# Rotating images by 180 degrees: the first group's load as four transfers of every fourth partition

## The chip, the core and the metric

The kernel runs on one core of one Trainium2 chip. The time is that of the device, in microseconds (us), for one execution; the number compared is the median over runs. A core has compute engines (of which this kernel uses DVE, the vector engine) and sixteen DMA engines that move data between the chip's main memory and the on-chip memory of 128 partitions. Transfers are issued by instructions on SP or on ACT, each of which has a DMA queue of its own; in the profile SP's queue is q1 and ACT's is q10.

## What is computed

Each of 32 x 3 images of 256 x 256 float32 values is turned by 180 degrees:

```python
def reference(x):            # x: (32, 3, 256, 256) float32
    return np.rot90(x, k=2, axes=(-2, -1)).astype(np.float32)
```

As an image lies in memory as 65,536 consecutive values, turning it by 180 degrees is reversing the order of these values. Nothing is calculated; 25.17 MB are read and 25.17 MB are written.

## The kernel before

The 96 images form three groups of 32 (G = 32). Each image is cut into four quarters of E = 16,384 values, so that a group is a tile of 128 partitions x 16,384 values: partition 4n + s holds quarter s of image n. The groups have one tile each, A, Bt and Ct, all resident at once, and there is a scratch tile T of 128 x 2,048.

A quarter is reversed inside its partition by DVE. `swap(t, lo, w)` (line 61) exchanges a stretch of w values at the front with the one at the mirrored place, both reversed, by three copies over T (all through line 52). `inside(t)` does a whole tile with four swaps of J = 2,048. The four quarters of an image must also change places; that is done by the store, whose destination has the quarter index reversed (line 58), so a store has the outer dimensions 32 (images) x 4 (quarters, reversed).

The order of the work is that of the program text:

1. Loads (lines 71 to 75): the first 512 values of every partition of A by ACT, the other 15,872 by SP, then all of Bt and all of Ct by SP. `load` (line 54) is one transfer of 128 rows.
2. DVE reverses most of A: three swaps of 2,048 and one of J - LAST = 896 (lines 78 to 80).
3. SP issues a short store of A's first LEAD = 128 columns (line 81), which are then final.
4. DVE reverses Bt (line 82) and then the remaining LAST = 1,152 values of each half of A (line 83).
5. SP issues the stores of the rest of A and of Bt; DVE reverses Ct; SP issues the store of Ct (lines 84 to 87).

Every store waits on SP for the DVE copies before it, and transfers of one queue are served in the order of issue. The lead store stands in SP's queue behind the load of Ct. The copies are kept in program order; the first copy of a swap reads the end of a partition and the second its front.

Of the kernel before, what the change touches and what calls it, by code (L numbers as in the profile page):

```python
# [2 lines left out]

os.environ.setdefault("NEURON_RT_ULTRASERVER_MODE", "4")

# [4 lines left out]


@with_exitstack
def kernel(
    ctx: ExitStack,
    tc: tile.TileContext,
    x: bass.AP,
    out: bass.AP,
):

    nc = tc.nc
    P = 128

    B, C, H, W = x.shape
    L = H * W
    G = 32
    E = L // 4
    J = E // 8

    x4 = x.rearrange("b c h w -> (b c) (h w)").rearrange(
        "(g n) (s e) -> g (n s) e", n=G, s=4)
    o4 = out.rearrange("b c h w -> (b c) (h w)").rearrange(
        "(g n) (s e) -> g n s e", n=G, s=4)  # L40

    pool = ctx.enter_context(tc.tile_pool(name="slots", bufs=1))
    A = pool.tile([P, E], x.dtype, tag="A")
    Bt = pool.tile([P, E], x.dtype, tag="B")
    Ct = pool.tile([P, E], x.dtype, tag="C")
    T = pool.tile([P, J], x.dtype, tag="T")

    def back(t, lo, hi):
        return t[:, hi - 1:(lo - 1 if lo else None):-1]

    def copy(dst, src):
        tc.keep_in_program_order(nc.vector.tensor_copy(out=dst, in_=src))  # L52

    def load(t, g, lo, hi, queue=nc.sync):
        return queue.dma_start(out=t[:, lo:hi], in_=x4[g][:, lo:hi])  # L55

    def store(t, g, lo, hi):
        return nc.sync.dma_start(
            out=o4[g][:, ::-1, lo:hi], in_=t[:, lo:hi])

    def swap(t, lo, w):
        hi = E - lo - w
        copy(T[:, 0:w], back(t, hi, hi + w))
        copy(t[:, hi:hi + w], back(t, lo, lo + w))
        copy(t[:, lo:lo + w], T[:, 0:w])

    def inside(t):
        for lo in range(0, E // 2, J):
            swap(t, lo, J)

    HEAD = 512
    load(A, 0, 0, HEAD, nc.scalar)
    load(A, 0, HEAD, E)
    load(Bt, 1, 0, E)
    load(Ct, 2, 0, E)
    LAST = 1152
    LEAD = 128
    for lo in range(0, E // 2 - J, J):
        swap(A, lo, J)
    swap(A, E // 2 - J, J - LAST)  # L80
    store(A, 0, 0, LEAD)
    inside(Bt)
    swap(A, E // 2 - LAST, LAST)
    store(A, 0, LEAD, E)
    store(Bt, 1, 0, E)
    inside(Ct)
    store(Ct, 2, 0, E)


# [1 line left out]
_INS = ['x']  # L91
_OUTS = [((32, 3, 256, 256), 'float32')]


# [23 lines left out]
```

## Time and profile before

| what | us |
|---|---|
| median of 3 runs (lowest, highest) | 121.94 (121.89, 122.06) |
| the profiled execution, own time | 122.03 |
| its span, from the first to the last instruction | 120.2 |
| DVE busy | 44.6 |
| issue of A's loads on SP and ACT | 0.73 |
| first copy on A | 22.68 |
| first copy on Bt | 42.10 |
| first copy on Ct | 61.50 |

The span is shorter than the execution's time, as the latter holds what comes before the first and after the last instruction. The profile lists for each DMA queue the packets, the bytes and the time that the packets took as a share of sixteen engines' span. Windows are stretches of the span with the busy time of DVE, the granted clock, the DMA share and the GB/s moved; as the bytes of a packet are counted where it ends, a short window can show more than the engines can move. The chain of waits follows the work that ended last back to what released it. The trace also has one record for each DMA packet with its start, duration, size and queue.

### The profile page before, as it was taken

What the parts mean: (1) busy time and instruction counts of PE and PEld (TensorE: products, weight loads), DVE (VectorE), ACT (ScalarE), POOL (GpSimd) and SP (SyncE); (2) the same over time, 40 slices, a digit from 0 to 9 for tenths busy, and PEclk for the clock granted to TensorE, in tenths of its full rate; (3) what the DMA queues carried; (4) which work ended last, traced back from release to release, by engine and by line L of the source; (5) the groups of instructions that cost most, each with busy time, mean ns of one, the idle gap of its engine ahead of it and who ended that gap; (6) DMA issues with size and microseconds to landing.
All of it is one profiled execution on the core that took longest, in us unless ns stands there. A gap on an engine that the chain in (4) does not pass through costs nothing.

```text
span 120.2 us, 98 instructions
## 1 busy us (share of the span) xinstructions
DVE 44.6 (37%) x39; POOL 0.2 (0%) x4
## 2 busy tenths in 40 slices
DVE  0000000499990099999759999400000000000000
POOL 0000000000000000000000000000000000000000
DMA  9888988899889988998889777988898889888980
GB/s 338 349 349 349 698 349 349 360 654 392 349 349 610 436 349 349 589 458 349 349 368 692 346 346 346 692 349 349 349 698 349 349 349 698 349 349 349 676 371 0
DMA packets 1152, 50.33 MB, mean 419 GB/s; under 512 B 128, under 2 KB 256, under 8 KB 384
## 3 DMA queue, kind: packets, MB, share of 16 engines
q1 hardware_dynamic: 1008, 50.07, 96.7%
q10 hardware_dynamic: 144, 0.26, 0.6%
HBM read 25.17 MB, written 25.17 MB: 419 GB/s over the span
## 4 chain that ended last, share of the span: by engine, by line
DMA 34%; DVE 27%; another core or an unknown queue 2%; issue 1%; SPq 0%; DVEq 0%
DMA Bt<-in_x_dram 34%; DVE T L52 9%; DVE Bt L52 8%; DVE Ct L52 8%; DVE A L52 1%; SPq L55 0%; DVEq L52 0%
## 5 line engine op out<-in xcount | busy, mean ns | idle before, releaser
L52 DVE COPY T<-A 128x2048 f32<-128x2048 f32 (+2 forms) x5 | 5.1, 1014 | 22.8 <-DMA A<-in_x_dram 22.7
L52 DVE COPY T<-Bt 128x2048 f32<-128x2048 f32 x4 | 4.9, 1227 | 6.2 <-DMA Bt<-in_x_dram 6.1
L52 DVE COPY T<-Ct 128x2048 f32<-128x2048 f32 x4 | 4.9, 1227 | 2.0 <-DMA Ct<-in_x_dram 1.9
L52 DVE COPY A<-T 128x2048 f32<-128x2048 f32 (+2 forms) x5 | 5.1, 1013 | 0.2
L52 DVE COPY A<-A 128x2048 f32<-128x2048 f32 (+2 forms) x5 | 5.1, 1013 | 0.2
L52 DVE COPY Bt<-T 128x2048 f32<-128x2048 f32 x4 | 4.9, 1227 | 0.1
L52 DVE COPY Ct<-T 128x2048 f32<-128x2048 f32 x4 | 4.9, 1227 | 0.1
L52 DVE COPY Bt<-Bt 128x2048 f32<-128x2048 f32 x4 | 4.9, 1226 | 0.1
L52 DVE COPY Ct<-Ct 128x2048 f32<-128x2048 f32 x4 | 4.9, 1226 | 0.1
L102 POOL MEMSET const-bfloat16-1.0<- 128x1 bf16 x1 | 0.1, 103 | 0.0
L102 POOL MEMSET const-uint8-127<- 128x1 uint8 x1 | 0.1, 103 | 0.0
L102 POOL MEMSET const-float32-1.0<- 128x1 f32 x1 | 0.1, 100 | 0.0
L102 POOL MEMSET const-float32-0.0<- 128x1 f32 x1 | 0.1, 99 | 0.2 <-issue 0.2
## 6 DMA issues: line engine op xcount, KB each, us to landing
out_dram<-A SPq DMA_DIRECT2D x1, 8128.0 KB, 21.2
A<-in_x_dram SPq DMA_DIRECT2D x1, 7936.0 KB, 21.9
A<-in_x_dram ACTq DMA_DIRECT2D x1, 256.0 KB, 22.1
out_dram<-A SPq DMA_DIRECT2D x1, 64.0 KB, 35.2
Bt<-in_x_dram SPq DMA_DIRECT2D x1, 40.8
Ct<-in_x_dram SPq DMA_DIRECT2D x1, 59.8
out_dram<-Bt SPq DMA_DIRECT2D x1, 39.9
out_dram<-Ct SPq DMA_DIRECT2D x1, 42.8
```

The lines of the kernel that those rows point to most:

```text
L52: tc.keep_in_program_order(nc.vector.tensor_copy(out=dst, in_=src))
L102: nc = _bacc.Bacc("TRN2", target_bir_lowering=False, num_devices=1)
```

## The change

The two loads of A by columns are replaced by four transfers by rows. Transfer i (0 to 3) takes the rows i, i + 4, i + 8 and so on, 32 whole rows of 16,384 values, into the partitions of the same numbers; that is quarter i of every image. Transfers 0 and 2 are issued by SP, 1 and 3 by ACT. The loads of Bt and Ct, the copies and the stores stay as they are.

```diff
-    HEAD = 512
-    load(A, 0, 0, HEAD, nc.scalar)
-    load(A, 0, HEAD, E)
+    SPLIT = 4
+    for i in range(SPLIT):
+        (nc.sync, nc.scalar)[i % 2].dma_start(
+            out=A[i::SPLIT, :], in_=x4[0][i::SPLIT, :])
     load(Bt, 1, 0, E)
     load(Ct, 2, 0, E)
```

In the built program SP then has four load issues ahead of its first store instead of three, and ACT two instead of one. The first copy on A waits for all four transfers (before: for the one by SP, and the second copy for the one by ACT), and so does the lead store; the store of the rest of A waits for DVE alone. All other instructions and their order are the same.

## The prediction

> **What bounds the kernel now.** I read the page's slices first, then the DMA queues, then windows cut at the moments where transfers land, and the chain of waits last.
>
> ```profile
> span 120.2 us, 98 instructions
> DVE 44.6 (37%) x39; POOL 0.2 (0%) x4
> DMA  9888988899889988998889777988898889888980
> ...
> q1 hardware_dynamic: 1008, 50.07, 96.7%
> q10 hardware_dynamic: 144, 0.26, 0.6%
> ```
>
> The only engine that computes is busy for 37% of the span, while packets fill 96.7% + 0.6% of the sixteen DMA engines' time, with zero only in the last slice. The windows (length, DVE busy, clock, DMA share, GB/s) show that nothing slackens between stages:
>
> ```profile
> 5.30:22.70 17.40, 0.02 (x1) 0.00 (x0) 1.00 1.00 431
> 22.70:42.00 19.30, 12.90 (x12) 0.00 (x0) 1.00 1.00 435
> 42.00:61.40 19.40, 17.00 (x15) 0.00 (x0) 1.00 1.01 435
> 61.40:80.80 19.40, 14.72 (x12) 0.00 (x0) 1.00 0.99 429
> 80.80:100.10 19.30, 0.00 (x0) 0.00 (x0) 1.00 1.00 435
> ```
>
> One packet is one row. At 435 GB/s an engine gets 27.2 GB/s, so a row of 65,536 bytes takes 2.41 us; the trace's packet records give a median of 2.418 us. They also give 2.342 us for the 63,488-byte rows of A, 0.084 us for the 2,048-byte heads and 2.401 us for the 65,024-byte rows of A's store. An engine carries 8 rows of each group. Its whole load is 8 x (2.342 + 0.084) + 16 x 2.418 + 8 x (0.027 + 2.401) + 16 x 2.418 = 116.2 us. The first packet starts at 1.77 us; the first rows end between 4.78 and 5.27 us (so the slowest engine is 5.27 - 1.77 - 2.34 = 1.16 us behind an ideal start); the last row of all ends at 119.09, its semaphore arrives at 119.44, and the end of the program follows at 120.2. 1.77 + 1.16 + 116.2 = 119.1: the end is the start of the slowest engine's stream plus its bytes.
>
> ```profile
> 1.18 40.84 DMA Bt<-in_x_dram
> ...
> 59.59 1.82 another core or an unknown queue
> ```
>
> In the chain of waits B's transfer ends at 42.02 (1.18 + 40.84). From there to 59.59 DVE reverses B and the rest of A (15 copies). Then SP issues A's store: 0.63 us of issue, with its first packet at 60.82. The engines finish C between 60.46 and 61.06 and then move the short lead store. So this store arrives just in time: the slowest engine is free at 61.26, 0.44 us after the first packet could start. Whatever delays B by more than that without delaying C becomes a gap.
>
> **The change, part by part.** The durations are of the profiled execution: 122.03 us with a span of 120.2, so 1.8 us lie around the span. The median of the runs is 121.94, 0.09 lower.
>
> Issues: on SP one issue (0.39 us) becomes two, so those of B and C move back by one step (1.18 to 1.65, 1.65 to 2.12). B's rows are not reached before about 21.8 us, where its first packet starts now: some 19 us of A's rows hide the 0.47. Without that cover it would cost 0.47. On ACT one issue (0.38) becomes two; ACT has nothing behind them.
>
> ```profile
> 0.73 0.38 ACTq L55 DMA_DIRECT2D A<-in_x_dram  x1
> 0.73 0.39 SPq L55 DMA_DIRECT2D A<-in_x_dram  x1
> 1.18 0.43 SPq L55 DMA_DIRECT2D Bt<-in_x_dram  x1
> ```
>
> Bytes: none added, none removed. If each new transfer gives each DMA engine 32/16 = 2 rows, an engine gets 4 x 2 x 2.418 = 19.34 us of A instead of 8 x 2.426 = 19.41: -0.07. Two more transfers add two semaphore writes per engine of 0.009 us: +0.02. Sum -0.05.
>
> Interleaving: half of A's rows now stand in ACT's queue. The records show what an engine does with two queues: after its first row it takes one head from q10, then one row from q1, in turn, eight times, at a period of 2.419 us, so turning costs nothing visible. A would then be complete after eight rows, at about 22.7 as now, and B after sixteen, at 42.0. If ACT's rows lag one turn behind, A is complete one row later (+2.42), and the stall goes no further: DVE's 12 copies for A end at 36.0 and it then stands idle for 6.1 us until B.
>
> ```profile
> DVE T L52 <- DMA A<-in_x_dram: 22.7, 1, 22.7
> DVE T L52 <- DMA Bt<-in_x_dram: 6.1, 1, 6.1
> ```
>
> Waits: DVE's first copy waits for four transfers instead of one, and so does the lead store on SP; behind that lead store stand only stores, and A's is ready at 59.6. Cost 0, covered by the same 6.1 us.
>
> Start: this is the part the trace does not show, since no transfer of 32 rows is in it. From below: today each engine gets eight rows from SP's first transfer before the queue is served further; with two rows there is less to hand out first. If all engines started as the quickest did (4.78 instead of 5.27) it is -0.49; with no lag at all, 2.34 after the first packet, -1.16. From above: if some engine got its first row only from the second issue of a queue, it would be 0.45 later (1.18 against 0.73). I take -0.10, near to zero, since the nearest row is the present first transfer and both its issue and its first addresses stay.
>
> Pace of the four transfers: how 32 rows at every fourth partition are dealt to sixteen engines is unseen too. The two nearest rows are the load of B (128 rows, 2.418 a row) and the stores, whose outer dimension in memory is 32 (2.401 to 2.42 a row): both at full pace, which gives +0. The other bound: every engine gets two rows, but pairs of engines meet on one path into the memory, one row each, in step. Then a row takes 4.84 and A 38.7 instead of 19.3: +19.3 at most; about 0.3 less at each of three changes of path, as an engine that is ahead by the spread of the starts (up to 0.49) uses the free one: +18.4. I take +0, from the stores, whose 32-long dimension is the more like.
>
> Sum: -0.05 - 0.10 + 0 = -0.15 on 122.03, that is 121.88 for such an execution and 121.8 against the median.
>
> [...]
>
> **Rivals.**
> (a) Two engines to a path, the whole of A at half pace: 121.9 + 18.4 = 140.3. For it: a transfer with an outer size of 32 on both sides is not in the trace, and the full pace of every present transfer leaves no spare (435 GB/s in each window) for a worse deal. Against: the stores, with 32 outside, have full pace. It decides as soon as A lands after about 28.8 (22.7 + 6.1), since DVE's gap is then gone; but the bytes queued behind are late from the first slowed row on, so every us counts in full.
> (b) A quicker start: rows of sixteen engines handed out sooner, -0.3 to -1.1, so 120.8 to 121.6. For it: six of the sixteen engines start their first packet 0.2 to 0.9 us after the tenth. Against: those late ones take only 2.34 to 2.93 us for it while the early ones take 2.96 to 3.36, so something other than the hand-out may set the 4.78 to 5.27.
> (c) A later start: two queues ask for full rows at once, one engine falls back up to 0.45, and B's landing, which sets A's store, with it: 122.2 to 122.4.
> (d) No effect: the removal of 0.07 us of heads is all there is, 121.9.
>
> **How the numbers follow.** That the rows keep their pace has 0.65: the forecast, 121.8, with a range of its own from 121.0 to 122.5. Within it, quicker by (b) 0.30, no difference 0.22, later by (c) 0.13. Rival (a), with partly slowed forms between, has 0.35, from what the trace cannot show. A measurement of this kernel can tell about 0.2%, 0.24 us, from no change. So faster 0.30, same 0.22, slower 0.13 + 0.35 = 0.48. The range has to reach to (a): 121.2 to 141.4 (121.9 + 19.3, and a little), which leaves out the quickest starts and no more.
>
> **What would show it.** Queue q10 should have 64 + 32 = 96 packets and 4.19 MB, q1 1008 - 144 + 96 = 960. If the forecast holds: A lands at 22.2 to 22.8, the window to 22.7 shows 430 GB/s or more, B lands at 42.0 +- 0.5 and the copies for A's rest end at 59.6 +- 0.5. If (a): under 250 GB/s up to about 41 us and DVE's first wait near 41. If (b) or (c): every landing from A on is displaced by one and the same amount. The prediction is wrong in its sum if A lands in time and the end is displaced all the same, which would be a gap between the loads and A's store.

## The result and the profile after

| | before | after |
|---|---|---|
| median (lowest, highest) of 9 runs each, us | 122.00 (121.89, 122.32) | 122.34 (122.19, 122.71) |
| profiled execution: own time, us | 122.03 | 122.30 |
| its span, us | 120.2 | 120.5 |

The ratio after to before is 1.0031, with a 95% interval of 1.0019 to 1.0042: the change makes the kernel 0.3% slower. That is little, but the interval does not reach 1.

The page of the changed kernel first: the span, the busy share of the DMA engines in 40 slices, then queue, packets, MB and share for the two queues.

```profile
span 120.5 us, 101 instructions
...
DMA  9888998899889988998889777988898889888980
...
q1 hardware_dynamic: 960, 46.14, 88.5%
q10 hardware_dynamic: 96, 4.19, 8.6%
```

The change does what it says: half of A's rows now run in ACT's queue, and together the packets fill 97.1% of the DMA engines' time (97.3% before). So the engines are as full as before, and the windows of the changed kernel (length, DVE busy, clock, DMA share, GB/s) confirm it:

```profile
5.30:22.70 17.40, 0.00 (x0) 0.00 (x0) 1.00 1.06 460
22.70:42.00 19.30, 12.92 (x12) 0.00 (x0) 1.00 1.00 435
42.00:61.40 19.40, 17.00 (x15) 0.00 (x0) 1.00 0.99 425
61.40:80.80 19.40, 14.72 (x12) 0.00 (x0) 1.00 1.02 440
80.80:100.10 19.30, 0.00 (x0) 0.00 (x0) 1.00 1.00 435
```

The 460 and 440 beside 425 are rows that end just inside one window instead of its neighbour; the whole packets of A's load have a median of 2.42 us in both queues, as B's have. No stage runs slower. What differs is when it starts. The order of time in the changed kernel's first microseconds (start, duration, queue, transfer, count):

```profile
0.73 1.19 ACTq L73 DMA_DIRECT2D A<-in_x_dram  x2
0.73 1.45 SPq L73 DMA_DIRECT2D A<-in_x_dram  x2
2.22 0.62 SPq L55 DMA_DIRECT2D Bt<-in_x_dram  x1
2.89 0.47 SPq L55 DMA_DIRECT2D Ct<-in_x_dram  x1
23.28 1.23 DVE L52 COPY T<-A 128x2048 f32<-128x2048 f32 x1 [23.28 <-DMA A<-in_x_dram]
```

Two issues take 1.45 us on SP, where before one took 0.39 and the next 0.43. The instructions of that line one by one (shortest, median and longest, in ns):

```profile
L73 ACTq DMA_DIRECT2D A<-in_x_dram x2: 538/578/617, 0.7 to 1.3; - x2
L73 SPq DMA_DIRECT2D A<-in_x_dram x2: 575/701/827, 0.7 to 1.4; - x2
```

By the packet records the first packet starts at 2.06 us instead of 1.77, and the slowest engine ends its first row at 5.72 instead of 5.27. Of these 0.45 us, 0.08 is the longer first row (65,536 bytes instead of 63,488), which the missing heads give back within A. The rest passes through: the last row of B ends 0.36 later (41.61 to 41.97), that of C 0.22 later (61.06 to 61.29; before, one row of C on the slowest engine took 2.55 instead of 2.42), the last packet of all 0.24 later (119.09 to 119.33). The waits and the chain of the changed kernel show the same displacement in DVE:

```profile
DVE T L52 <- DMA A<-in_x_dram: 23.3, 1, 23.3
DVE T L52 <- DMA Bt<-in_x_dram: 5.8, 1, 5.8
...
2.22 40.09 DMA Bt<-in_x_dram
...
59.89 1.81 another core or an unknown queue
```

A is waited for until 23.3 instead of 22.7, which only shortens the idle time before B; B lands at 42.31 (2.22 + 40.09) instead of 42.02, and the copies ahead of A's store end at 59.89 instead of 59.59. In DVE everything from B on is 0.3 us late; in the packet records it is between 0.22 and 0.36.

### The profile page after: what moved, and what is told of

It reads as the page before. It is cut to its first block, busy times and chain, and to the rows that moved or that the text cites. A ratio compares the mean times of both kernels' runs of the same rounds, so it can differ in the third digit from the quotient of the medians.

```text
span 120.5 us, 101 instructions
## 1 busy us (share of the span) xinstructions
DVE 44.6 (37%) x39; POOL 0.2 (0%) x4
## 4 chain that ended last, share of the span: by engine, by line
DMA 33%; DVE 27%; another core or an unknown queue 1%; SPq 1%; issue 1%; DVEq 0%
DMA Bt<-in_x_dram 33%; DVE T L52 9%; DVE Bt L52 8%; DVE Ct L52 8%; DVE A L52 1%; SPq L73 1%; DVEq L52 0%
## 5 line engine op out<-in xcount | busy, mean ns | idle before, releaser
L52 DVE COPY T<-A 128x2048 f32<-128x2048 f32 (+2 forms) x5 | 5.1, 1014 | 23.4 <-DMA A<-in_x_dram 23.3
## 6 DMA issues: line engine op xcount, KB each, us to landing
out_dram<-A SPq DMA_DIRECT2D x1, 8128.0 KB, 21.1
```

## The experiments

All kernels differ from the changed one in A's load alone. "Plain" is a load of all 128 partitions, "stepped" one of every fourth (or second) partition. Where the table speaks of the first large packet, it is the first of 16 KB or more in the packet records of the one profiled execution; the difference is that of the medians against the runs of before on the same chip.

| A's load | first issue, us | first large packet, us | median, us | difference, us | ratio (95%) |
|---|---|---|---|---|---|
| changed kernel | 0.58 SP, 0.54 ACT | 2.06 | 122.34 | +0.34 | 1.0031 (1.0019, 1.0042) |
| one plain load | 0.39 | 1.74 | 122.12 | +0.18 | 1.0029 (1.0015, 1.0043) |
| neighbouring rows | 0.40, 0.41 | 1.75 | 143.03, two runs | +21.1 | 1.1731 (1.1710, 1.1752) |
| four stepped, all on SP | 0.58 | 2.08 | 122.56 | +0.62 | 1.0049 (1.0036, 1.0062) |
| two stepped of 64 rows | 0.59, 0.54 | 2.07 | 122.35 | +0.41 | 1.0035 (1.0022, 1.0047) |
| plain first, then stepped | 0.37, 0.53 | 1.73 | 121.93 | -0.05 | 0.9996 (0.9987, 1.0005) |
| stepped on the chip only | 0.58, 0.55 | 2.08 | 122.52 | +0.54 | 1.0050 (1.0035, 1.0065) |
| stepped in memory only | 0.40, 0.41 | 1.75 | 143.01, one run | +21.0 | none |
| four by columns | 0.38, 0.39 | 1.74 | 122.06 | +0.08 | 1.0014 (1.0000, 1.0029) |
| plain first, then plain | 0.38 | 1.74 | 121.84 | -0.17 | 0.9992 (0.9983, 1.0001) |
| tiny stepped one first | 0.58 | 2.55 | 122.93 | +0.92 | 1.0078 (1.0065, 1.0090) |
| short head first, on SP | 0.39 | 2.68 (heads from 1.76) | 122.00 | -0.01 | 0.9999 (0.9990, 1.0008) |

### Is it the shape of the transfers, or their two queues?

One load of 128 whole rows on SP, nothing on ACT:

```diff
-    for i in range(SPLIT):
-        (nc.sync, nc.scalar)[i % 2].dma_start(
-            out=A[i::SPLIT, :], in_=x4[0][i::SPLIT, :])
+    load(A, 0, 0, E)
```

> A is loaded by one transfer of 128 whole rows on SP, nothing on ACT. Shape theory (a transfer of 32 rows at every fourth partition takes longer to hand out: 0.55 to 0.58 us of issue instead of 0.39, so the first packet comes at 2.06 us instead of 1.77): first issue 0.38 to 0.43 us, first packet at 1.75 to 1.82 us, time within 0.15 us of before. Two-queue theory (full rows asked for by two queues at once hold each other up): the same, since there is one queue. Whole-row theory (rows of 65,536 bytes instead of 63,488 start later): first packet near 2.06 us, 0.3 us slower than before.

The four stepped transfers, all on SP:

```diff
-        (nc.sync, nc.scalar)[i % 2].dma_start(
+        nc.sync.dma_start(
```

> The four transfers of every fourth partition, all issued by SP. Shape theory: first issue 0.55 us or more, first packet near 2.06 us, 0.3 us slower than before. Two-queue theory: first issue 0.39 us, first packet near 1.77 us, time within 0.15 us of before. Should the later issues take 0.6 to 0.8 us each, they are hidden by the rows in flight (two rows, 4.84 us, for each transfer), so B's packets still follow A's without a gap.

The plain load's issues, the second being B's:

```profile
0.73 0.39 SPq L55 DMA_DIRECT2D A<-in_x_dram  x1
1.18 0.42 SPq L55 DMA_DIRECT2D Bt<-in_x_dram  x1
```

Its first packet starts at 1.74. With one queue only, the four stepped transfers are long to issue all the same (ns, shortest, median, longest):

```profile
L73 SPq DMA_DIRECT2D A<-in_x_dram x4: 577/586/594, 0.7 to 2.6; - x4
```

The two-queue theory has fallen: with ACT left out, the first packet is late (2.08) and the time is worse, not better. The whole-row theory has fallen too as far as the first packet goes: whole rows start at 1.74. But the plain load was expected within 0.15 us of before and is 0.18 slower, and its ratio of 1.0029 (1.0015, 1.0043) can't be told from the change's 1.0031 (1.0019, 1.0042). Its runs are uneven: six of the eleven lie between 122.05 and 122.12, the others reach up to 122.91. So something besides the step is in the result, and these runs alone don't say how much of the change's 0.34 the step makes; the last group below returns to it.

Two transfers of 64 rows, `SPLIT = 2`:

> Two transfers of 64 rows at every second partition, one by SP and one by ACT. Shape theory: first issues 0.5 us or more if any step costs (first packet 2.0 to 2.06 us, 0.2 to 0.3 us slower than before), or half of that if the cost goes by the number of transfers. Two-queue theory: as with the change, 0.3 us slower than before. If the rows of such a transfer are dealt so that engines meet on a path, A lands at up to 41 us and the time rises to up to 141 us.

```profile
L73 SPq DMA_DIRECT2D A<-in_x_dram x1: 588/588/588, 0.7 to 0.7; - x1
L73 ACTq DMA_DIRECT2D A<-in_x_dram x1: 542/542/542, 0.7 to 0.7; - x1
```

A first issue of 0.59 on SP and a first packet at 2.07. The price does not grow with the transfer: on SP 64 rows at a step of two take 0.59, 32 at a step of four 0.58; on ACT both take 0.54. The plain issue of B behind it, at 1.36, takes 0.82, the longest of any plain issue here. The rows keep their pace at this step also: A is waited for until 23.2, with the change until 23.3.

In time, the kernels that open with a stepped transfer were expected 0.2 to 0.3 us slower than before, and came out 0.41 (two of 64 rows), 0.62 (four on SP) and, below, 0.54 (stepped on the chip only) slower. The first packet's 0.3 is thus not all of their loss.

### Which step, and what would the other split have cost?

Neighbouring rows into neighbouring partitions:

```diff
-            out=A[i::SPLIT, :], in_=x4[0][i::SPLIT, :])
+            out=A[32 * i:32 * i + 32, :], in_=x4[0][32 * i:32 * i + 32, :])
```

> Four transfers of 32 neighbouring rows into 32 neighbouring partitions, by SP and ACT in turn. Shape theory, if it is the step of four partitions that costs: issue 0.39 us and first packet near 1.77 us; if it is the number of rows or of transfers: issue 0.55 us, first packet near 2.06 us, as with the change. Pace, by the rival of the prediction (engines that meet on one path): A at half pace, landing near 41 us, time near 141 us, or worse; if paths do not matter: 2.42 us a row, A landing near 23 us, time 122.3 us.

The instructions of its load, then its windows and its first wait:

```profile
L73 ACTq DMA_DIRECT2D A<-in_x_dram x2: 409/428/446, 0.7 to 1.2; - x2
L73 SPq DMA_DIRECT2D A<-in_x_dram x2: 395/400/406, 0.7 to 1.2; - x2
```

```profile
10.00:20.00 10.00, 0.00 (x0) 0.00 (x0) 1.00 1.02 210
20.00:30.00 10.00, 0.00 (x0) 0.00 (x0) 1.00 1.01 210
```

```profile
DVE T L52 <- DMA A<-in_x_dram: 44.3, 1, 44.3
```

This split is quick to issue, with a first packet at 1.75, and then moves 210 GB/s instead of 435: the records show 5.12 us a row, more than twice 2.42. The DMA share of 1.02 shows that full engines alone don't tell the pace; the packets are only longer. Why a row takes longer there no run shows. In this kernel SP and ACT issue partitions 0 to 31 and 32 to 63 first, at 0.7, and 64 to 95 and 96 to 127 behind them, at 1.2; from issue to landing the four take from 23.0 to 42.9 us. Another order over the two queues was not run.

Each side's step alone, the chip's and then the memory's:

```diff
-            out=A[i::SPLIT, :], in_=x4[0][i::SPLIT, :])
+            out=A[i::SPLIT, :], in_=x4[0][32 * i:32 * i + 32, :])
```

> The four transfers write every fourth partition, but each reads 32 neighbouring rows of memory, so the quarters and images of the first group land in other places of the output. If the step on the chip's side costs the issue time: first issues 0.54 to 0.58 us, first packet 2.06 us, time as with the change (0.3 us slower than before). If the step on the memory's side costs it: 0.39 to 0.41 us, first packet 1.75 us, 122.0 to 122.15 us. Pace in both cases 2.42 us a row if the partitions written set it.

```diff
-            out=A[i::SPLIT, :], in_=x4[0][i::SPLIT, :])
+            out=A[32 * i:32 * i + 32, :], in_=x4[0][i::SPLIT, :])
```

> The mirror of the one before: 32 neighbouring partitions are written, from every fourth row of memory, so the quarters and images of the first group land in other places of the output. Step on the chip's side costs: first issues 0.39 to 0.41 us, first packet 1.75 us; step on the memory's side costs: 0.54 to 0.58 us, 2.06 us. Pace: 5.12 us a row and 143 us in all, if the partitions written set it; 2.42 us a row if the rows read do.

The load's instructions with the step on the chip only:

```profile
L73 SPq DMA_DIRECT2D A<-in_x_dram x2: 583/698/813, 0.7 to 1.4; - x2
L73 ACTq DMA_DIRECT2D A<-in_x_dram x2: 547/580/613, 0.7 to 1.3; - x2
```

and with the step in memory only:

```profile
L73 SPq DMA_DIRECT2D A<-in_x_dram x2: 395/400/406, 0.7 to 1.2; - x2
L73 ACTq DMA_DIRECT2D A<-in_x_dram x2: 409/428/446, 0.7 to 1.2; - x2
```

Both prices belong to the partitions that are written. A step there costs 0.14 to 0.19 us of the first issue and 0.3 us of the first packet (2.08 against 1.75); neighbouring partitions in four pieces cost half the pace (143.03 and 143.01 us in all, against 122.52 with the step on the chip). Which rows of memory are read makes no difference to either here.

### Is the start all of it?

A plain transfer of 4,096 columns ahead of the stepped ones:

```diff
+    FIRST = 4096
+    load(A, 0, 0, FIRST)
     for i in range(SPLIT):
         (nc.sync, nc.scalar)[i % 2].dma_start(
-            out=A[i::SPLIT, :], in_=x4[0][i::SPLIT, :])
+            out=A[i::SPLIT, FIRST:E], in_=x4[0][i::SPLIT, FIRST:E])
```

> SP first issues a plain transfer of A's first 4,096 columns for all 128 partitions, then the four transfers of every fourth partition carry the other 12,288 columns, by SP and ACT in turn. Step theory (only the hand-out of the first stepped transfer matters, as everything later is hidden behind rows in flight): first issue on SP 0.39 us, first packet 1.72 to 1.80 us, time 121.9 to 122.15 us, as with one plain load. Rival (stepped transfers cost something all along, by their number or their two queues): slower than before by 0.3 us or more, as with the change.

The same with a plain second transfer, `load(A, 0, FIRST, E)`, in place of the four:

> As the run with a plain first transfer, but the other 12,288 columns come by one plain transfer on SP: no step anywhere, no ACT. If stepped transfers cost nothing once rows are in flight: the same as that run within 0.15 us (121.8 to 122.1 us), first packet 1.72 to 1.80 us. If they do cost something later: 0.2 us or more quicker than that run.

The first of them in order of time:

```profile
0.73 0.37 SPq L55 DMA_DIRECT2D A<-in_x_dram  x1
0.74 1.18 ACTq L75 DMA_DIRECT2D A<-in_x_dram  x2
1.16 1.20 SPq L75 DMA_DIRECT2D A<-in_x_dram  x2
```

Three quarters of A are still stepped and the issues are still long, but the first packet starts at 1.73 and the loss is gone: 0.9996 (0.9987, 1.0005). That does not give the loss to the step alone: this kernel also opens with short rows, and one plain load of whole rows, without a step, was slower than before too. With the step away altogether the ratio is 0.9992 (0.9983, 1.0001); the two intervals overlap, and the medians are 0.12 us apart against their own before, inside the 0.15 expected. So behind rows in flight stepped transfers cost nothing that these runs can tell.

The suspected cost made larger, with little of A stepped:

```diff
-    for i in range(SPLIT):
-        (nc.sync, nc.scalar)[i % 2].dma_start(
-            out=A[i::SPLIT, :], in_=x4[0][i::SPLIT, :])
+    TINY = 128
+    nc.sync.dma_start(out=A[0::4, 0:TINY], in_=x4[0][0::4, 0:TINY])
+    load(A, 0, TINY, E)
+    for i in (1, 2, 3):
+        nc.sync.dma_start(out=A[i::4, 0:TINY], in_=x4[0][i::4, 0:TINY])
```

> SP first issues one stepped transfer of 32 x 128 values, then one plain transfer of A's other 16,256 columns, then three more stepped transfers of 32 x 128. Start theory: the stepped issue (0.58 us, next issue 0.63 us later) goes ahead of the plain one, so the first large packet starts at 2.35 to 2.45 us, 0.6 us later than with one plain load, and the end moves by the same: 122.6 to 122.8 us. Rival (the change costs by stepped rows in flight, not by the start): only 2% of A is stepped, so 122.0 to 122.2 us.

```profile
0.73 0.58 SPq L72 DMA_DIRECT2D A<-in_x_dram  x1
1.35 0.57 SPq L55 DMA_DIRECT2D A<-in_x_dram  x1
1.97 1.77 SPq L75 DMA_DIRECT2D A<-in_x_dram  x3
```

One tiny stepped transfer of 16 KB ahead of a plain load makes the kernel 0.92 us slower than before; the plain load alone was 0.18 slower, and the two intervals don't meet. Its first large packet starts at 2.55 instead of 1.74, 0.81 later. The slowest engine's first large row ends 0.65 later (6.18 against 5.53), and the last packet of all 0.64 later (119.82 against 119.18): from the first row on, the end follows one to one. Start and time are both above what was expected (2.35 to 2.45 and 122.6 to 122.8); of the start's excess 0.15 is seen in the lines, where the plain issue behind a stepped one took 0.57 instead of 0.42. The rows need not be large or many for the step to cost.

Not all of this is the step's. The next issue comes 0.62 us later behind the tiny stepped transfer (1.35 against 0.73) and 0.45 later behind a plain one (1.18 against 0.73), so by estimate 0.45 would be the price of any transfer ahead; no kernel with a tiny plain one was run.

### What the plain load lacks

The number and the queues without a step, four transfers by columns:

```diff
-        (nc.sync, nc.scalar)[i % 2].dma_start(
-            out=A[i::SPLIT, :], in_=x4[0][i::SPLIT, :])
+        load(A, 0, i * E // SPLIT, (i + 1) * E // SPLIT,
+             (nc.sync, nc.scalar)[i % 2])
```

> Four transfers of A by columns, 128 partitions x 4,096 each, by SP and ACT in turn: the number of transfers and the two queues of the change without its step. Step theory: issues 0.38 to 0.43 us, first packet 1.72 to 1.80 us, time within 0.2 us of the one plain load of A (121.95 to 122.3 us). If number or two queues cost: 122.3 us or more with a first packet near 2.06 us.

Before's two loads, the short head on SP too (`load(A, 0, 0, HEAD)` and `load(A, 0, HEAD, E)`):

> Before's two loads of A, both on SP: 512 columns first, then 15,872. Start theory: first packets at 1.72 to 1.80 us, but they are short (0.084 us each, 0.7 us for eight), and the second issue comes 0.45 us later, so its rows are there at about 2.2 us, before the short ones are done at 2.5 us: time 121.8 to 122.1 us. Rival (what before had over one plain load was its second queue): 122.1 us or more.

Four transfers over two queues cost 0.08 us, at the edge of what can be told. Before's head on SP gives before's time, though its large rows start only behind the heads, at 2.68 instead of the 2.2 to 2.5 expected; so before's second queue was worth nothing by itself. Between the kernel that opens with 64 KB rows and no step (one plain load, +0.18) and those that open with short or split ones (-0.17 to +0.08), 0.1 to 0.35 us are left that are no matter of the first packet: it starts at 1.73 to 1.77 in all of them. The gap is clear between the plain load and "plain first, then plain", whose intervals don't meet, but not between the plain load and the four by columns. Short first packets are not what before has over the plain load: it opens with rows of 63,488 bytes, and by the packet records its heads start only at 4.78. In the one trace of the plain load the slowest engine ends its first row 3.80 us after the first packet, before's 3.51 (3.58 for a full row); in the kernels with stepped first rows it is 3.62 to 3.83. Why a first row of 64 KB ends later on the slowest engine was not tried.

## Why the prediction was right and wrong

**The bound: right.** The end is the start of the slowest engine's stream plus its bytes. In the packet records of the six kernels that open with rows of 65,024 or 65,536 bytes at full pace, the last packet ends 113.61 to 113.73 us after the slowest engine's first row, whether that row ends at 5.53 (one plain load) or at 6.18 (tiny stepped one first).

**Pace and bytes: right.** A sum of -0.05 for the bytes was forecast; from the slowest engine's first row to its last byte of A the changed kernel needs 16.91 us instead of 17.01, and 0.08 of that difference had been paid in the longer first row, so some 0.02 were gained. The pace was taken as +0, and the rows kept 2.42 us. Rival (a), pairs of engines on one path, does not hold at every fourth partition. A loss of its size does come with neighbouring partitions, 21 us instead of the 18.4 to 19.3 worked out, and it goes by the partitions written; that engines meet in pairs there is not seen in the records. Two more transfers cost little: four by columns took 0.08 more than before.

**Interleaving, waits, the late issue of B: right in cost.** B was issued at 2.22 instead of the 1.65 forecast, and the first copy on A started 0.6 later (A's last byte came 0.35 later, at 22.63 against 22.28); rows in flight (B's first packet starts at 22.01) and DVE's idle time (5.8 us until B) hid both. ACT's rows went first, from 2.06, and SP's from 5.09; no run shows that this matters.

**The start: wrong, and with it the direction.** The step that failed reads "I take -0.10, near to zero, since the nearest row is the present first transfer and both its issue and its first addresses stay". The issue does not stay: 0.58 instead of 0.39 on SP, because of the partitions' step, and the first packet follows 0.77 to 0.80 us after the end of a stepped issue against 0.62 after the plain load's. In place of -0.10 the runs showed +0.29 on the first packet and, on the slowest engine's first row, +0.37 beyond the 0.08 of its greater length. Both are below the bound of +0.45, but on the other side of zero from the value taken. Only 0.24 reached the last packet, since one row of C before happened to take 0.13 longer. The argument that two rows instead of eight leave less to hand out also fell: 64 rows at a step are no dearer than 32, and 32 neighbouring rows (0.40) no cheaper than 128 (0.39).

**The rival that came true is (c)**, a later start that B's landing and A's store share: 122.2 to 122.4 was given, 122.34 measured, with a chance of 0.13. Its cause was put wrongly: with one queue the first packet is as late, and what delays it is the step. So that its number fits is in part luck. The step is also not the whole cause: one plain load of whole rows, without a step, loses 0.18 of the 0.34 by medians, and nearly all of it by ratios (1.0029 against 1.0031). Only the traces, one of each, tell the two apart: the changed kernel's slowest first row ends 0.19 later than the plain load's, its last packet 0.15 later. How the two parts add in the changed kernel's time is not settled.

## What to carry to other kernels

This kernel's DMA engines never rest (97.1% and 97.3% full), and a late first row of the slowest engine was paid for one for one: 0.65 us in that row were 0.64 in the last packet (tiny stepped one first against one plain load). The lowest medians came with a plain first transfer of short rows over all 128 partitions (4,096 columns: 121.84 and 121.93), and stepped transfers behind it cost nothing that could be told (0.9996 against 0.9992 of before). To see what a split of a load costs, read the issue time of its instructions, the start of the first packet and the end of the slowest engine's first row, not only GB/s; the first packet alone misleads, as the short head first on SP shows, whose large packets start at 2.68 and whose time is before's. And where 32 rows had to go alone, every fourth partition kept the full pace, 2.42 us a row, where 32 neighbours took 5.12.

## What was not expected of the hardware

- A transfer that steps over partitions on the chip takes 0.53 to 0.59 us to issue as the first of its queue, against 0.37 to 0.41 for plain ones; it is a price for the transfer (128 values a row or 16,384, 32 rows or 64), and the plain issue behind it is slowed too (0.57 to 0.82 instead of 0.42 or 0.43).
- Four transfers of neighbouring partitions run at 210 GB/s while the DMA share stays at 1.02: 5.12 us a row, 0.28 more than twice the usual 2.42.
- The time from the last packet to the end of the span grows with the number of transfers in the program, by one trace of each kernel: 1.12 us with seven, 1.15 to 1.16 with eight, 1.18 to 1.21 with ten and 1.26 to 1.27 with eleven. What fills it was not tried; it makes 0.02 of the change's 0.27 in the profiled executions.
